# A two-layer transformer block on one core: the experts' TensorE order pinned, weight splits of 2048 columns in three buffers

## The chip, the cores and the metric

The kernel runs on one core of a Trainium2 chip. The metric is the device time of one execution in microseconds (us), as the median of several runs. A NeuronCore has five engines that run side by side and wait for one another through semaphores: PE (TensorE, matrix products), DVE (VectorE), ACT (ScalarE), POOL (GpSimd) and SP (SyncE, which here only starts transfers). Transfers run on 16 DMA engines.

## The reference

Two layers over 256 tokens of 1024 features, all in fp32. Layer 0 is a stick-breaking attention and a dense SwiGLU of 2816 hidden features; layer 1 is a block attention (with 256 tokens there is one block, so it is a causal softmax with a relative bias) and a mixture of 8 experts, top 2, each a SwiGLU of 3584 hidden features. Cut to its core:

```
for i in range(2):
    hn = rmsnorm(h, mixer_norm[i]);  q, k, v = heads(hn @ w_qkv[i])
    o = stick_breaking_attention(q, k, v) if i == 0 else moba_attention(q, k, v, rel_bias)
    h = h + o @ w_o[i]
    hn = rmsnorm(h, ffn_norm[i])
    if i == 0: h = h + (silu(hn @ w1) * (hn @ w3)) @ w2
    else:      # gates: softmax over the two largest of hn @ router
        h = h + sum_e gate[:, e] * ((silu(hn @ e_w1[e]) * (hn @ e_w3[e])) @ e_w2[e])
return rmsnorm(h, final_norm)
```

## The kernel before, in words

**Three products for one.** TensorE multiplies in a reduced form of fp32. To keep fp32 accuracy each weight is split in two: ACT copies it into the reduced form (L154, `wh`) and DVE subtracts that from the weight (L155, `wl`). `mm3` (L175 to 179) then makes three matmuls: L176 `wh` by the high part of the data, L177 `wl` by the high part, L178 `wh` by the low part. The data are the stationary operand, the weights stream through as 512 columns. The data are split in the same way by `split_out` (L182 on ACT, L183 on DVE).

**The weights' way.** A list `jobs` holds all weights in the order of use, as granules of 128 x 2048 elements (1 MB). SP loads them into a ring of buffers (`RING` = 9 and, in the expert stage, 7 more that other stages have freed). `stream` takes a loaded granule, makes the two splits in pieces of `HALF` = 1024 columns, and yields 512-column slices to `mm3`. The pieces lie in a pool `split` with four buffers for `wh` and four for `wl`. A buffer is written again when the last matmul that reads it is done, and a ring slot is loaded again when its split is done. Weights that take a norm's factor (`g` not None: qkv and the dense w1 and w3) are split 512 columns at a time by L162 and L163.

**An expert.** Its rows (at most 128 are computed here, the rest is left to code behind a branch at the end) pass through 7 chunks of 512 hidden features, so the stage has 56 chunks. A chunk, by the loop at the end of the listing, is: w1, two granules (called G0 and G1 below), into one bank; w3, two granules (G2, G3), into another; ACT's silu (L587) and DVE's product (L588) make the hidden tile `nat`; and the w2 product (`down`) of the chunk before, two granules (G4, G5). Before that product `hid_t` turns the hidden tile of the chunk before by four transposes (L599), and `split_out` writes it into the single pair of buffers `hts`. A chunk is thus 72 matmuls of 512 columns and 4 transposes. At the last chunk of an expert `turn_x` adds 8 transposes (L876) with a split of the next expert's rows, and in the first chunk of the next one `store_y` copies the result out (ACT L859, DVE L860). In the last expert `fetch` gathers the others' results and `add_rows` (L847, four instructions of 1024 columns on DVE) adds them to `h`.

**Who sets the order.** The Tile framework's scheduler lays out each engine's queue from the dependences; `behind` adds an order without a semaphore where the author wants one. Each engine then works its queue strictly in order. In the experts before, nothing but the scheduler says where the transposes L599 stand among TensorE's matmuls.

**Ahead of the experts** stands the routing: after the last `w_o` matmul, `h` gets the attention's output (L534), TensorE turns it (L287) and multiplies by the router (L695), with copies on ACT (L742) and DVE (L740), the router's logits leave the bank by L704, and a chain of small DVE steps up to L714 and L865 gives the order in which TensorE gathers each expert's rows (L887).

## Time and profile before

| | |
|---|---|
| runs, median (lowest to highest) | 1440.25 us (1438.56 to 1440.41), 3 runs |
| the profiled execution: its time, its span | 1438.46 us, 1436.8 us |
| granted TensorE clock over the span | 0.996 |
| PE busy | 1417.6 us, 99% of the span |
| DVE, ACT, POOL busy | 1170.2 us (81%), 1010.3 us (70%), 45.3 us (3%) |
| moved by DMA | 442.11 MB, 308 GB/s in the mean |

A row of the timeline gives the start (us from the span's start), the time of the row, engine, line, operation, what is written from what, tile and data type, and how many instructions the row takes together. Behind it, in brackets, stands the time for which the engine had been idle and the instruction that ended the wait. Since matmuls are pipelined, the time between two starts tells more than the time of one. The share of busy time is a mean: the experts take 960 of the 1437 us, and what one wait there costs is read from that stage.

### The profile page before, as it was taken

The numbers are of one execution on the slowest core, as the hardware profiler recorded it, in microseconds if no ns is written. First come the engines' busy times: TensorE is split into PE (matmuls) and PEld (weight loads), VectorE is DVE, ScalarE is ACT, GpSimd is POOL, SyncE is SP. The second block draws the span as 40 slices with busy tenths as digits, with TensorE's granted clock in tenths as the row PEclk, the third lists the DMA queues.
The fourth block names the chain that finished last, engine by engine and source line by source line (L and its number), as shares of the span: only waits on it lengthen the run. The fifth ranks groups of instructions, "written<-read, shape, count | busy, mean of one in ns | idle before, by whom it ended". The sixth has DMA issues, their size and how long they took to land. (4 is left out here: it accounts for less than half of the span.)

```text
span 1436.8 us, 19637 instructions
## 1 busy us (share of the span) xinstructions
PE 1417.6 (99%) x7285; PEld 1176.7 (82%) x7285; DVE 1170.2 (81%) x1384; ACT 1010.3 (70%) x1282; POOL 45.3 (3%) x71
## 2 busy tenths in 40 slices
PE   9999999999999999999999999999999999999997
PEld 7877999988877888888888888878878887887775
DVE  6656766667667999999999988888888888898887
ACT  6656655546655778878878777777777777777765
POOL 1000000000001000000000000000000000000200
PEclk9999999999999999999999999999999999999998
DMA  9633865556566999999999999999999999999850
GB/s 353 236 117 108 303 196 186 186 173 228 180 246 218 402 401 388 385 373 373 388 392 362 391 362 373 366 381 368 354 389 372 357 380 380 358 374 369 320 189 32
DMA packets 172153, 442.11 MB, mean 308 GB/s; under 512 B 7299, under 2 KB 9395, under 8 KB 157972
## 3 DMA queue, kind: packets, MB, share of 16 engines
q1 hardware_dynamic: 166852, 422.61, 80.6%
q0 software_dynamic: 5136, 18.18, 3.5%
q8 instruction: 59, 0.97, 0.3%
q14 instruction: 42, 0.34, 0.1%
q10 hardware_dynamic: 64, 0.02, 0.0%
HBM read 430.00 MB, written 11.03 MB: 307 GB/s over the span
## 5 line engine op out<-in xcount | busy, mean ns | idle before, releaser
L155 DVE TENSOR_TENSOR wl<-raw,wh 128x1024 fp32r<-128x1024 f32 x710 | 834.4, 1220 | 112.9 <-ACT wh L154 106.0
L154 ACT ACTIVATE wh<-raw 128x1024 fp32r<-128x1024 f32 x710 | 725.6, 1057 | 133.9 <-PE bank L178 97.7
L177 PE MATMUL bank<-wl,oh_t 128*128 128x512 f32 x968 | 382.9, 396 | 2.9 <-DVE wl L155 2.0
L176 PE MATMUL bank<-wh,oh_t 128*128 128x512 f32 x968 | 375.5, 393 | 2.1 <-ACT wh L154 1.6
L178 PE MATMUL bank<-wh,oh_t 128*128 128x512 f32 x904 | 353.5, 391 | 0.1
L177 PEld LDWEIGHTS bank<-wl,oh_t 128*128 128x128 f32 x968 | 181.9, 188 | 60.0 <-DVE wl L155 18.9
L176 PEld LDWEIGHTS bank<-wh,oh_t 128*128 128x128 f32 x968 | 182.2, 188 | 41.4 <-ACT wh L154 1.8
L178 PEld LDWEIGHTS bank<-wh,oh_t 128*128 128x128 f32 x904 | 170.2, 188 | 34.1 <-DVE oh_t L183 0.8
L178 PE MATMUL bank<-wh,ol_t 128*128 128x512 f32 x504 | 194.6, 392 | 0.0
L162 ACT ACTIVATE wh<-raw,gcol 128x512 fp32r<-128x512 f32 (+1 forms) x192 | 123.8, 698 | 87.4 <-PE bank L318 56.3
L163 DVE SCALAR_TENSOR_TENSOR wl<-raw,gcol,wh 128x512 fp32r<-128x512 f32 (+1 forms) x192 | 131.1, 725 | 65.8 <-ACT wh L162 65.3
L177 PE MATMUL bank<-wl,ol_t 128*128 128x512 f32 x440 | 174.7, 397 | 0.4 <-DVE wl L155 0.4
L318 PE MATMUL bank<-x_h,wh 128*128 128x256 f32 x512 | 143.8, 282 | 0.0
L318 PE MATMUL bank<-x_h,wl 128*128 128x256 f32 x512 | 142.9, 280 | 0.0
L318 PE MATMUL bank<-x_l,wh 128*128 128x256 f32 x512 | 142.7, 279 | 0.0
L176 PE MATMUL bank<-wh,ol_t 128*128 128x512 f32 x440 | 137.1, 393 | 0.0
L178 PEld LDWEIGHTS bank<-wh,ol_t 128*128 128x128 f32 x504 | 94.4, 188 | 19.9 <-issue 1.1
L318 PEld LDWEIGHTS bank<-x_h,wh 128*128 128x128 f32 x512 | 95.9, 188 | 1.9 <-issue 1.1
L177 PEld LDWEIGHTS bank<-wl,ol_t 128*128 128x128 f32 x440 | 83.0, 189 | 16.4 <-DVE wl L155 0.6
L318 PEld LDWEIGHTS bank<-x_h,wl 128*128 128x128 f32 x512 | 96.1, 188 | 0.0
L318 PEld LDWEIGHTS bank<-x_l,wh 128*128 128x128 f32 x512 | 95.9, 187 | 0.2
L176 PEld LDWEIGHTS bank<-wh,ol_t 128*128 128x128 f32 x440 | 81.6, 188 | 16.8
(218 smaller groups left out, 1106.1 us busy)
## 6 DMA issues: line engine op xcount, KB each, us to landing
raw<-in_e_w_dram SPq DMA_DIRECT2D x335, 1024.0 KB, 7.3
raw<-in_w_dram SPq DMA_DIRECT2D x33, 1024.0 KB, 5.1
raw<-in_w_qkv_dram SPq DMA_DIRECT2D x22, 1024.0 KB, 5.7
raw<-in_w_o_dram SPq DMA_DIRECT2D x8, 1024.0 KB, 7.5
xs_d<-hn POOLq DMA_DIRECT2D x1, 4096.0 KB, 16.0
xr<-xs_d POOLq DMA_DIRECT2D x7, 512.0 KB, 7.5
ys_d<-yr POOLq DMA_DIRECT2D x7, 512.0 KB, 7.8
raw<-in_w_qkv_dram SPq DMA_DIRECT2D x4, 512.0 KB, 6.8
```

The source lines that it names most:

```text
L154: i0 = nc.scalar.activation(wh[:, :m], src, AF.Copy)
L155: i1 = nc.vector.tensor_sub(wl[:, :m], src, wh[:, :m].bitcast(F32))
L162: i0 = nc.scalar.activation(wh[:, cs], src[:, cs], AF.Copy, scale=gc)
L163: i1 = nc.vector.scalar_tensor_tensor(wl[:, cs], src[:, cs], gc, wh[:, cs].bitcast(F32), op0=ALU.mult, op1=ALU.subtract)
L176: i0 = nc.tensor.matmul(ps, s[0], m[0], start=start, stop=False)
L177: nc.tensor.matmul(ps, s[0], m[1], start=False, stop=False)
L178: i1 = nc.tensor.matmul(ps, s[1], m[0], start=False, stop=stop)
L318: nc.tensor.matmul(to, w[a][:, ms], z[:, :, c], start=c + i + m % 2 == 0, stop=c == NC - 1 and m % 2 == 1 and i == 2, skip_group_check=True)
```

## The change

The order of TensorE in the experts is written with `behind`: each group of matmuls is placed after the last of the group before (`last`), so that the order of a chunk is w1, the four transposes, w3, (the turn of the next rows), w2. Weights without a norm factor (`w_o`, the dense w2, all of the experts') are split in pieces of 2048 columns, a granule at once, and the pieces lie in three tiles of 2048 columns for `wh` and three for `wl`; weights with a factor still go in halves of such a tile. The ring gives up two slots for it. All other queues (ACT, DVE, POOL, SP) are still laid out by the scheduler. Lines move: L154 and L155 become L166 and L167, L176 to L178 become L188 to L190, L182 and L183 become L194 and L195, L587 and L588 become L599 and L600, L599 becomes L611, L847 becomes L864 and L860 becomes L877.

```diff
--- before.py
+++ after.py
@@ -30,9 +30,10 @@
 BIG = 1e30
 N_BUCKETS = 32
 MAX_DISTANCE = 128
-RING = 9
+RING = 7
 RING1, RING2, RING3 = 1, 3, 3
 GRAN = 2048
+SPLITS = 3
 HALF = GRAN // 2
 NV = 384
 WARM = 6
@@ -50,7 +51,19 @@
 
     const = ctx.enter_context(tc.tile_pool(name="const", bufs=1))
     ring = ctx.enter_context(tc.tile_pool(name="ring", bufs=RING))
-    split = ctx.enter_context(tc.tile_pool(name="split", bufs=4))
+    split = ctx.enter_context(tc.tile_pool(name="split", bufs=1))
+    highs, lows = ([split.tile([P, GRAN], F32R, name=f"{n}{i}") for i in range(SPLITS)]
+                   for n in ("wh", "wl"))
+    n_split = [0]
+
+    def next_split(m):
+
+        if n_split[0] % GRAN + m > GRAN:
+            n_split[0] += -n_split[0] % GRAN
+        at, i = n_split[0] % GRAN, n_split[0] // GRAN
+        n_split[0] += m
+        return [x[i % SPLITS][:, at:at + m] for x in (highs, lows)]
+
     act = ctx.enter_context(tc.tile_pool(name="act", bufs=1))
     small = ctx.enter_context(tc.tile_pool(name="small", bufs=2))
     psp = ctx.enter_context(tc.tile_pool(name="psp", bufs=1, space=PSUM))
@@ -144,11 +157,10 @@
             t = loaded[n_used[0]]
             _, nk, fn = jobs[n_used[0]]
             n_used[0] += 1
-            k = min(nk, HALF // fn)
+            k = min(nk, (GRAN if g is None else HALF) // fn)
             for c0 in range(0, nk, k):
-                wh = split.tile([P, HALF], F32R, name="wh")
-                wl = split.tile([P, HALF], F32R, name="wl")
                 m = k * fn
+                wh, wl = next_split(m)
                 src = t[:, c0 * fn:c0 * fn + m]
                 if g is None:
                     i0 = nc.scalar.activation(wh[:, :m], src, AF.Copy)
@@ -592,18 +604,23 @@
                                            op1=ALU.mult)
         return t
 
-    def hid_t(t, n, ps, a, c, apart=True):
+    def hid_t(t, n, ps, a, c, apart=True, after=None):
         k = n // P
         tv = t[:, :n].rearrange("p (f j) -> p j f" if apart else "p (j f) -> p j f", j=k)
         for j in range(k):
-            nc.tensor.transpose(ps[:, j * P:(j + 1) * P], tv[:, j], ident)
+            i0 = nc.tensor.transpose(ps[:, j * P:(j + 1) * P], tv[:, j], ident)
+            if after is not None:
+                behind((i0, after))
+                after = i0
         split_out(ps[:, :n], a[:, :n], c[:, :n])
         return [(a[:, j * P:(j + 1) * P], c[:, j * P:(j + 1) * P]) for j in range(k)]
 
-    def down(ps, hT, j, w, start, stop):
+    def down(ps, hT, j, w, start, stop, after=None):
         for half in range(2):
-            mm3(ps[half], hT[j], tuple(a[:, half * FC:(half + 1) * FC] for a in w),
-                start and j == 0, stop and j == len(hT) - 1)
+            i0, i1 = mm3(ps[half], hT[j], tuple(a[:, half * FC:(half + 1) * FC] for a in w),
+                         start and j == 0, stop and j == len(hT) - 1)
+            behind((i0, after))
+        return i1
 
     def dense_ffn(pool, hold, then):
         y = [[bank[0], bank[1]], [bank[2], bank[7]]]
@@ -933,7 +950,7 @@
                 i1 = nc.vector.tensor_add(ht[b][:, hs], ht[b][:, hs], ps)
         return i0, i1
 
-    pend, done, added = None, None, None
+    pend, done, added, last = None, None, None, None
     gather((3, 4), raws[2])
     k = 0
     most_v = None
@@ -947,15 +964,18 @@
                 if bk == b3:
                     held[:] = None, None
                 for c, w in enumerate(stream(NC, hold=held)):
-                    _, last = mm3(bank[bk], (eh[:, c], el[:, c]), w, c == 0, c == NC - 1)
+                    i0, i1 = mm3(bank[bk], (eh[:, c], el[:, c]), w, c == 0, c == NC - 1)
+                    behind((i0, last))
+                last = i1
                 if pend is not None and bk == b1:
-                    hT = hid_t(pend[1], FC, bank[pend[2]], *hts)
+                    hT = hid_t(pend[1], FC, bank[pend[2]], *hts, after=last)
             if i == len(ecs) - 1 and e + 1 < NE:
                 turn_x(xr, (2, 7), last)
             t = gate_mul(ep.tile([P, FC], F32, name="nat"), bank[b1], bank[b3], n, after=added)
             if pend is not None:
                 for j, w in enumerate(stream(4)):
-                    down(y, hT, j, w, pend[0] == 0, pend[0] == len(ecs) - 1)
+                    i1 = down(y, hT, j, w, pend[0] == 0, pend[0] == len(ecs) - 1, last)
+                last = i1
             pend = (i, t, b1)
             if i == 0:
                 if e:
```

The order of TensorE in one chunk, before: `ol_t` is the turned hidden tile of the w2 product, bank_76 and bank_77 take its result.

```order
L177 MATMUL bank_76<-wl,ol_t 128x512
L178 MATMUL bank_76<-wh,ol_t 128x512
L177 MATMUL bank_77<-wl,ol_t 128x512
L178 MATMUL bank_77<-wh,ol_t 128x512
L176 MATMUL bank_76<-wh,ol_t 128x512
L176 MATMUL bank_77<-wh,ol_t 128x512
L599 MATMUL bank_79<-ident,nat 128x128 x4
L177 MATMUL bank_76<-wl,ol_t 128x512
L178 MATMUL bank_76<-wh,ol_t 128x512
L177 MATMUL bank_77<-wl,ol_t 128x512
```

After, at the same place of the program (bank_87 is the w1 product, bank_88 the w3 product):

```order
L189 MATMUL bank_87<-wl_69,oh_t 128x512
L190 MATMUL bank_87<-wh_66,oh_t 128x512
L611 MATMUL bank_85<-ident,nat 128x128 x4
L188 MATMUL bank_88<-wh_67,oh_t 128x512
L189 MATMUL bank_88<-wl_70,oh_t 128x512
L190 MATMUL bank_88<-wh_67,oh_t 128x512
L188 MATMUL bank_88<-wh_67,oh_t 128x512
```

The four transposes stood among the w2 product of the chunk before; now they stand between w1 and w3 of the same chunk.

DVE's order in a chunk of the later experts, before: each raw buffer (a granule) gives two pieces, and the product L588 stands between the two pieces of the first w2 granule and those of the second.

```order
L155 TENSOR_TENSOR wl_10421<-raw_10061,wh_10420 128x1024
L155 TENSOR_TENSOR wl_10431<-raw_10061,wh_10430 128x1024
L588 TENSOR_TENSOR nat_10415<-nat_10415,bank6_82 128x512
L155 TENSOR_TENSOR wl_10443<-raw_10089,wh_10442 128x1024
L155 TENSOR_TENSOR wl_10453<-raw_10089,wh_10452 128x1024
L155 TENSOR_TENSOR wl_10465<-raw_10111,wh_10464 128x1024
L155 TENSOR_TENSOR wl_10475<-raw_10111,wh_10474 128x1024
L183 TENSOR_TENSOR ol_t_90<-bank5_81,ol_t_90 128x512
L155 TENSOR_TENSOR wl_10487<-raw_10136,wh_10486 128x1024
```

After (wl0 to wl2 are the three tiles): the rows from G3 of a chunk to G0 of the next.

```order
L167 TENSOR_TENSOR wl0_68<-raw_8425,wh0_65 128x2048
L195 TENSOR_TENSOR ol_t_96<-bank3_85,ol_t_96 128x512
L167 TENSOR_TENSOR wl1_69<-raw_8441,wh1_66 128x2048
L600 TENSOR_TENSOR nat_8667<-nat_8667,bank6_88 128x512
L167 TENSOR_TENSOR wl2_70<-raw_8460,wh2_67 128x2048
L167 TENSOR_TENSOR wl0_68<-raw_8476,wh0_65 128x2048
```

A granule is one row now. From the third expert's fourth chunk on the product L600 stands ahead of the whole G5, as here, where in the chunks before it stands behind G5.

DVE's order around the last chunks of expert 7, before (L847 is `add_rows`):

```order
L155 TENSOR_TENSOR wl_12456<-raw_12094,wh_12455 128x1024
L155 TENSOR_TENSOR wl_12466<-raw_12122,wh_12465 128x1024
L847 SCALAR_TENSOR_TENSOR h0_84<-raw_12056,ex_4567,h0_84 128x1024
L155 TENSOR_TENSOR wl_12476<-raw_12122,wh_12475 128x1024
L847 SCALAR_TENSOR_TENSOR h0_84<-raw_12056,ex_4567,h0_84 128x1024
L588 TENSOR_TENSOR nat_12442<-nat_12442,bank6_82 128x512
L847 SCALAR_TENSOR_TENSOR h1_85<-raw_12064,ex_4567,h1_85 128x1024
L183 TENSOR_TENSOR ol_t_90<-bank5_81,ol_t_90 128x512
L155 TENSOR_TENSOR wl_12488<-raw_12144,wh_12487 128x1024
L847 SCALAR_TENSOR_TENSOR h1_85<-raw_12064,ex_4567,h1_85 128x1024
```

After, from G0 of the chunk before the last on; wl0 of raw_9884 is that chunk's G0, wl0 of raw_9954 its G3, raw_9916 G1 and raw_9932 G2:

```order
L167 TENSOR_TENSOR wl0_68<-raw_9884,wh0_65 128x2048
L864 SCALAR_TENSOR_TENSOR h0_90<-raw_9900,ex_4271,h0_90 128x1024 x2
L864 SCALAR_TENSOR_TENSOR h1_91<-raw_9908,ex_4271,h1_91 128x1024
L167 TENSOR_TENSOR wl0_68<-raw_9954,wh0_65 128x2048
L864 SCALAR_TENSOR_TENSOR h1_91<-raw_9908,ex_4271,h1_91 128x1024
L167 TENSOR_TENSOR wl1_69<-raw_9916,wh1_66 128x2048
L167 TENSOR_TENSOR wl2_70<-raw_9932,wh2_67 128x2048
```

And the last chunk, where raw_10005 is G0, raw_10021 G1, raw_10059 G3 and raw_10037 G2:

```order
L600 TENSOR_TENSOR nat_10194<-nat_10194,bank6_88 128x512
L167 TENSOR_TENSOR wl0_68<-raw_10005,wh0_65 128x2048
L167 TENSOR_TENSOR wl1_69<-raw_10021,wh1_66 128x2048
L167 TENSOR_TENSOR wl0_68<-raw_10059,wh0_65 128x2048
L167 TENSOR_TENSOR wl2_70<-raw_10037,wh2_67 128x2048
L167 TENSOR_TENSOR wl1_69<-raw_10075,wh1_66 128x2048
```

G3 moved ahead of G1 and G2 into the tile that G0 has just left, with three of the four additions ahead of it; in the last chunk G3 moved ahead of G2. ACT's queue has the same order of pieces. TensorE's has G0, G1, the transposes, G2, G3 in both chunks.

DVE in the routing before (sums, a norm's step, the copy of the turned rows, the logits):

```order
L534 TENSOR_TENSOR h0_84<-h0_84,bank0_76 128x512
L534 TENSOR_TENSOR h0_84<-h0_84,bank1_77 128x512
L534 TENSOR_TENSOR h1_85<-h1_85,bank2_78 128x512
L534 TENSOR_TENSOR h1_85<-h1_85,bank7_83 128x512
L277 TENSOR_SCALAR ms_4484<-ss_4482 128x1
L740 COPY hn1_148<-bank6_82 128x512
L704 COPY lg_3319<-bank0_76 128x8
```

After (L546, L289, L757 and L721 are L534, L277, L740 and L704):

```order
L546 TENSOR_TENSOR h0_90<-h0_90,bank0_82 128x512
L546 TENSOR_TENSOR h0_90<-h0_90,bank1_83 128x512
L546 TENSOR_TENSOR h1_91<-h1_91,bank2_84 128x512
L546 TENSOR_TENSOR h1_91<-h1_91,bank7_89 128x512
L167 TENSOR_TENSOR wl1_69<-raw_3846,wh1_66 128x2048
L757 COPY hn1_154<-bank6_88 128x512
L289 TENSOR_SCALAR ms_4188<-ss_4186 128x1
L721 COPY lg_3095<-bank0_82 128x8
```

The piece of raw_3846 (G2 of expert 0's first chunk) now stands between the sums and the copies; on ACT its `wh` stands ahead of the copies L759 (L742 of before).

## Rows read from the trace of the kernel before

**Rows 1.** The page, busy time of each engine and its share.

```profile
PE 1417.6 (99%) x7285; PEld 1176.7 (82%) x7285; DVE 1170.2 (81%) x1384; ACT 1010.3 (70%) x1282; POOL 45.3 (3%) x71
```

**Rows 2.** DVE timeline, the product L588: one in each chunk.

```profile
476.72 0.68 DVE L588 TENSOR_TENSOR nat<-nat,bank 128x512 f32<-128x512 f32 x1
...
629.17 0.68 DVE L588 TENSOR_TENSOR nat<-nat,bank 128x512 f32<-128x512 f32 x1
629.77 4.92 DVE L155 TENSOR_TENSOR wl<-raw,wh 128x1024 fp32r<-128x1024 f32 x4
...
646.01 0.68 DVE L588 TENSOR_TENSOR nat<-nat,bank 128x512 f32<-128x512 f32 x1
...
972.07 0.68 DVE L588 TENSOR_TENSOR nat<-nat,bank 128x512 f32<-128x512 f32 x1
...
989.22 0.68 DVE L588 TENSOR_TENSOR nat<-nat,bank 128x512 f32<-128x512 f32 x1
...
1354.48 0.69 DVE L588 TENSOR_TENSOR nat<-nat,bank 128x512 f32<-128x512 f32 x1 [1.77 <-PE bank L178]
...
1413.06 0.68 DVE L588 TENSOR_TENSOR nat<-nat,bank 128x512 f32<-128x512 f32 x1
```

**Rows 3.** ACT timeline, the chunk from 957 us on.

```profile
960.26 0.60 ACT L182 ACTIVATE ol_t<-bank 128x512 fp32r<-128x512 f32 x1 [1.95 <-PE bank L177]
```

**Rows 4.** Waits of the weight loads, 466 to 1413 us: total us, times, longest.

```profile
PEld bank L177 <- DVE wl L155: 19.3, 44, 1.1
```

**Rows 5.** Timeline of PE, PEld and DVE at one such wait.

```profile
961.84 1.23 DVE L155 TENSOR_TENSOR wl<-raw,wh 128x1024 fp32r<-128x1024 f32 x1 [0.26 <-ACT wh L154]
...
963.01 0.39 PE L176 MATMUL bank<-wh,oh_t 128*128 128x512 f32 x1
963.12 0.19 PEld L177 LDWEIGHTS bank<-wl,oh_t 128*128 128x128 f32 x1
963.24 0.40 PE L177 MATMUL bank<-wl,oh_t 128*128 128x512 f32 x1
```

**Rows 6.** PE timeline, the turn of the next expert's rows.

```profile
559.85 1.03 PE L876 MATMUL bank<-ident,xr 128*128 128x128 f32 x8
560.64 0.71 PE L176 MATMUL bank<-wh,ol_t 128*128 128x512 f32 x2
```

**Rows 7.** The costliest groups: busy us, mean ns, idle before and releaser.

```profile
L155 DVE TENSOR_TENSOR wl<-raw,wh 128x1024 fp32r<-128x1024 f32 x710 | 834.4, 1220 | 112.9 <-ACT wh L154 106.0
L154 ACT ACTIVATE wh<-raw 128x1024 fp32r<-128x1024 f32 x710 | 725.6, 1057 | 133.9 <-PE bank L178 97.7
```

**Rows 8.** PE and DVE timeline, the last w_o matmuls and the sums.

```profile
437.47 0.62 PE L178 MATMUL bank<-wh,ol_t 128*128 128x512 f32 x2
...
437.90 2.48 DVE L534 TENSOR_TENSOR h<-h,bank 128x512 f32<-128x512 f32 x4 [1.88 <-PE bank L178]
...
438.38 0.62 PE L178 MATMUL bank<-wh,ol_t 128*128 128x512 f32 x2
```

**Rows 9.** ACT and DVE timeline, the copies and the logits of the routing.

```profile
439.47 1.09 ACT L742 ACTIVATE hn<-bank 128x512 f32<-128x512 f32 x2 [3.91 <-PE bank L287]
...
442.75 0.17 DVE L704 COPY lg<-bank 128x8 f32<-128x8 f32 x1 [0.20 <-PE bank L695]
```

**Rows 10.** DVE timeline, an addition of rows in expert 7 and its successor.

```profile
1393.89 1.28 DVE L847 SCALAR_TENSOR_TENSOR h<-raw,ex,h 128x1024 f32<-128x1024 f32 x1
1395.08 0.68 DVE L588 TENSOR_TENSOR nat<-nat,bank 128x512 f32<-128x512 f32 x1
```

**Rows 11.** PE timeline, the longest wait of expert 7's end.

```profile
1398.19 0.50 PE L176 MATMUL bank<-wh,oh_t 128*128 128x512 f32 x1 [1.63 <-ACT wh L154]
```

**Rows 12.** Windows behind it: busy PE, PEld, DVE, ACT, POOL, PEclk, DMA.

```profile
1400.00:1402.00 2.00, 2.00 (x6) 1.17 (x5) 2.00 (x3) 1.47 (x3) 0.00 (x0) 0.52 0.00 0
1402.00:1404.00 2.00, 2.00 (x6) 1.63 (x7) 2.00 (x3) 0.57 (x1) 0.00 (x0) 0.63 0.00 0
```

**Rows 13.** SP's waits: us in total, times, longest one.

```profile
SPq L130 <- DVE wl L155: 863.7, 332, 10.0
```

## The prediction

> **What bounds the kernel now.** I read the page's busy times first: PE is busy for 1417.6 us, 99% of the span, DVE for 81% and ACT for 70% [rows 1]. A gain can come only from time in which TensorE stands still or runs slowly, so I looked next at how long a chunk of the experts takes. Its clock is the DVE product, one in each chunk [rows 2]. From 629.17 to 646.01 a chunk takes 16.84 us. The matmuls of one half product start 0.2275 us apart (four from 437.47 to 438.38 [rows 8]); 72 of them make 16.38, and with four transposes a chunk has nothing left to lose at 16.84. From 972.07 to 989.22 it takes 17.15 [rows 2]. The whole run of 54 chunks from 476.72 to 1413.06 takes 936.34; 54 x 16.84 are 909.36, so 27.0 us are lost there. This sum is what the change can work on.
>
> Where they go: seven turns of the next expert's rows belong to the work and stay. Eight transposes take 0.79 to the next matmul, and the two matmuls behind take 0.71 instead of 0.62, together 0.88 [rows 6]; seven are 6.2. The last three chunks, from 1354.48 to 1413.06, take 58.58 instead of 50.52: 8.1 lost [rows 2]. The other 12.7 lie mostly in the chunks of 17.15. There ACT waits 1.95 us with the split of the turned hidden tile [rows 3]: the transposes are done early, inside the w2 product of the chunk before, but the single buffer `hts` is read until that product's last matmul. What ACT splits behind it is late, then DVE, and in the end the weight load of the second product: 44 such waits, 19.3 us [rows 4].
>
> **Prices.** A 1024-column subtraction takes 1.22 us, ACT's copy 1.06 [rows 7]. The trace has no 2048-column one. Between the 512-column row of 0.68 [rows 2] and 1.22 lie 0.54 for 512 columns, so 1024 more cost 1.08 and a piece of 2048 takes 2.30. From above it is bounded by two pieces, 2.44; from below by four times the 0.54, 2.16, as if starting cost nothing. I take 2.30, the line through two rows. For ACT, 0.60 at 512 columns [rows 3] and 1.06 give 1.98. A DVE instruction lets its successor start about 0.09 before its end (0.68 after 0.60, 629.17 to 629.77 [rows 2]; 1.28 after 1.19 [rows 10]), so a piece holds the queue for 2.21. TensorE's last matmul lets DVE begin 0.43 after its start (437.47 to 437.90 [rows 8]). DVE's piece ends at 961.84 + 1.23 = 963.07 and the waiting weight load starts at 963.12, 0.05 later, which is 0.11 after the start of the matmul in front (963.01). The next matmul starts 0.23 after that one, as usual [rows 5]. So a weight load may come 0.11 late without cost, and beyond it every delay counts.
>
> **The order of TensorE.** With the transposes behind w1, the w2 product that read `hts` is over before them, so ACT's wait goes. What is late next is G5's low part, wherever L600 stands ahead of the whole G5 in DVE's queue. Let the last matmul of G3 start at 0. L600 starts at 0.43, G5's subtraction at 1.03, it ends at 3.33, the weight load can start at 3.38. G4's 12 matmuls and the first two of G5 start in between; the second of these two starts at 14 x 0.227 = 3.18, and the load may come until 3.29. It is 0.09 late. With a piece of 1024 columns the same step had 1.0 to spare. This holds for 32 chunks, from the third expert's fourth on, without the chunks that hold a turn, whose transposes give 0.88 of slack, and the last two: 32 x 0.09 = 2.9. In the earlier chunks L600 stands behind G5 and the cost is nothing.
>
> **Ends of experts.** In the same order two splits of the turned rows stand between G5 and the next G0 (2 x 0.60). G0's subtraction runs from 1.03 + 2.21 + 1.20 = 4.44 to 6.74, its load could start at 6.79. The matmul in front starts after 0.88 + 25 x 0.227 = 6.56, so the load is due at 6.67: 0.12 late. One chunk on, the copy out (L877) waits for the last w2 matmul (24 x 0.227 + 0.09 + 0.43 = 5.97), and G1's subtraction follows from 6.57 to 8.87, its load at 8.92; due is 37 x 0.227 + 0.09 + 0.11 = 8.60: 0.32 late. Five of the seven ends have this order: 5 x 0.44 = 2.2.
>
> **The routing.** ACT's copy of G2 waits for the last `w_o` matmul (438.61), so it runs from 439.04 to 441.02, ahead of the copy that started at 439.47 [rows 8, 9]. DVE's piece holds its queue from 441.06 to 443.27; then L757 (0.60) and a small step (0.08), and the logits are read at 443.95 instead of 442.75 [rows 9]. The chain behind them ends at the gathers, so TensorE begins the experts 1.2 later.
>
> **The end of expert 7.** G3 of the last chunk but one goes into the tile that G0 has left. Let G0's first matmul start at 0; its piece entered DVE's queue at -2.5 and leaves it at -0.3. Three additions of 1.19 [rows 10] end at 3.3 and are covered. ACT's copy for G3 waits for G0's last matmul (11 x 0.227 + 0.43 = 2.93), ends at 4.91; the subtraction holds DVE until 7.2, the fourth addition until 8.35, and only then G1's subtraction runs, until 10.65. TensorE wants it at 2.72 + 0.11: 7.8 us of standing still. In the last chunk G3 stands ahead of G2 in the same way. From the start of G0's last matmul on: 0.43, 1.98 on ACT, 2.21 for G3, 2.30 for G2 and 0.1 of signals make 7.0; G1 and the transposes cover 13 x 0.227 + 0.5 + 0.1 = 3.6: 3.4 us. After such a wait the clock falls: behind the 1.63 us wait and a further one [rows 11], 2 us at 0.52 and 2 us at 0.63 [rows 12], that is from the upper level of 2.4 GHz to 1.2 for most of 3.4 us, and 2 x 0.48 + 2 x 0.37 = 1.7 lost. I count it once. Together 12.9, against 8.1 now.
>
> The Trainium skill says of the clock (TensorE: Matmul & The Clock Gate, HAM oscillation) that every long enough wait throttles the array anew. By it the second wait would cost another 1.7; rows 11 and 12 agree for the first, and no row here shows two in turn.
>
> **What costs nothing.** Pieces of `w_o` and the dense w2 lie beside a TensorE that is idle for 19 us in the whole span [rows 1]; there is little to win in those stages, and I allow 1 us either way. Two ring slots less: SP waits 863.7 us, 332 times, for a split to free a slot [rows 13], so the ring is full ahead of use; 14 slots are some 39 us of work at 16.84 per six. If that cover were gone, each wait of TensorE for a load would show on L166.
>
> **Sum.** Of the 27.0, the turns keep 6.2. The other 20.8 go; 2.9 + 2.2 + 1.2 + 12.9 = 19.2 come. The profiled execution of 1438.46 becomes 1436.9. The median of the runs, 1440.25, stands 1.8 above that execution, the lowest run beside it. I place the median of the changed kernel between, at 1438.3: no change that can be told, since a measurement of this kernel tells about 0.2%, 2.9 us.
>
> **Rivals.** First, faster: the 0.09 is thin. If a piece takes 2.20 instead of 2.30, the 32 waits go (2.9), the ends cost 0.2 each less (1.2), the end of expert 7 some 0.4: 1433.8. A cheaper end of expert 7 works the same way, up to 4 us. For it speaks that 0.43 and 0.05 are single rows; against it, that 2.20 lies under the line of rows 2 and 7.
>
> The Trainium skill gives this rival a rule and its opposite (VectorE: DVE Perf Modes, The TRN2 errata): a fixed term of 58 cycles at 0.96 GHz in one table, which makes 2.19 of 2048 columns, and 151 measured for such a two-operand fp32 operation, which makes 2.29. For 1024 columns they give 1.13 and 1.22; the trace has 1.220 and decides for the second. I leave the first a tenth within this rival's chance.
>
> Second, slower: a piece costs as much as two, 2.44. Then G5 is 0.23 late, 32 times (4.5 more), G0 and G1 at the ends 0.28 more (1.4), the end of expert 7 some 0.6, the routing 0.1: 1444.9. It decides from about 2.40 on, where the sum passes 2.9 over the old median. Against it stands the same line; for it, that three buffers of a granule leave nothing to hide a late piece.
>
> Third, the order doesn't cure: the split of the hidden tile still waits for something else in the later experts and chunks stay at 17.15. Then the 12.7 don't go, the 2.9 don't come: 1448. Against it: the transposes come after the w2 product in TensorE's own queue.
>
> **How the numbers follow.** My forecast gets 0.38 (its own range 1436 to 1442), the first rival 0.37, the second 0.19, the third 0.06. So faster 0.37, within 0.2% 0.38, slower 0.25. The range takes in the first rival with the cheaper end, 1430, and the second with a little of the third, 1446.5.
>
> **What would show it.** Chunks of 16.84 in experts 0 and 1 and about 16.93 later; L167 at 2.30; ACT's L194 without its wait; a wait of TensorE of about 7 to 8 us in expert 7's last chunk but one on DVE's G1, another of 3 in the last. I am wrong if later chunks take 17 or more, if the end of expert 7 runs through, or if TensorE waits in the attention or the dense stage.

## The result: 1447.56 us, slower by half a per cent

The changed kernel takes 1447.56 us (median of four runs, 1443.66 to 1447.94) against 1439.40 of the kernel before in the same job (1438.18 to 1440.41): a ratio of 1.0052, interval 1.0039 to 1.0064. The forecast was 1438.3 with a range up to 1446.5. The profiled execution took 1447.67 us, its span 1445.9; before, span 1436.8. The 9.1 us between the spans are what has to be found. One of the four executions took 1443.66, with a granted clock of 0.993 over its span instead of 0.991, so what the clock costs differs from one to the next. (One execution of the last kernel below took 1749.17 us at a granted clock of 0.75; it belongs to the chip's slow state, and its ratio leaves it out.)

The page of the changed kernel, busy times and the two costliest groups (line, engine, operation, count | busy us, mean ns of one | idle before, releaser). Its L166 and L167 are L154 and L155 of before:

```profile
PE 1415.8 (98%) x7285; PEld 1181.5 (82%) x7285; DVE 1140.0 (79%) x1030; ACT 970.0 (67%) x928; POOL 46.2 (3%) x71
...
L167 DVE TENSOR_TENSOR wl<-raw,wh 128x2048 fp32r<-128x2048 f32 (+1 forms) x356 | 805.9, 2283 | 155.0 <-ACT wh L166 154.3
L166 ACT ACTIVATE wh<-raw 128x2048 fp32r<-128x2048 f32 (+1 forms) x356 | 676.4, 1914 | 261.7 <-PE bank L190 214.9
```

DVE and ACT are 30 and 40 us less busy than in [rows 1], because half as many split instructions start; the time is longer all the same. A piece costs 2.28 us on DVE and 1.91 on ACT, where 2.30 and 1.98 were forecast. Two pieces of 1024 cost 2.44 [rows 7].

**Where the 9.1 us are.** The experts are cut at the first matmul and at the DVE products (one in each chunk; L588 before [rows 2], L600 now). PE and DVE timeline of the changed kernel, the last `w_o` matmul, the first of the experts, the product that begins the last three chunks, and the last product:

```profile
440.30 0.39 PE L188 MATMUL bank<-wh,oh_t 128*128 128x512 f32 x1
...
455.08 0.50 PE L188 MATMUL bank<-wh,oh_t 128*128 128x512 f32 x1
...
1349.83 0.69 DVE L600 TENSOR_TENSOR nat<-nat,bank 128x512 f32<-128x512 f32 x1 [0.27 <-PE bank L190]
...
1417.28 0.68 DVE L600 TENSOR_TENSOR nat<-nat,bank 128x512 f32<-128x512 f32 x1
```

The same instants before were 437.92, 452.96, 1354.48 and 1413.06. So:

| stretch | before | after | difference | forecast |
|---|---|---|---|---|
| to the last high part of `w_o` (L176 before, L188 now) | 437.9 | 440.3 | +2.4 | 0 |
| routing, to the first expert matmul | 15.0 | 14.8 | -0.3 | +1.2 |
| chunks, to the last three | 901.5 | 894.8 | -6.8 | -7.6 |
| the last three chunks | 58.6 | 67.5 | +8.9 | +4.8 |
| from the last product to the end | 23.7 | 28.6 | +4.9 | 0 |

The differences are taken from the instants themselves, before rounding.

**The chunks** came out as worked out, though not for the reason given, as the experiments show. DVE timeline of the changed kernel, two products of expert 4, against [rows 2]:

```profile
972.74 0.69 DVE L600 TENSOR_TENSOR nat<-nat,bank 128x512 f32<-128x512 f32 x1 [0.28 <-PE bank L190]
973.35 6.69 DVE L167 TENSOR_TENSOR wl<-raw,wh 128x2048 fp32r<-128x2048 f32 x3
...
989.69 0.69 DVE L600 TENSOR_TENSOR nat<-nat,bank 128x512 f32<-128x512 f32 x1 [0.27 <-PE bank L190]
```

A late chunk takes 16.95 instead of 17.15. The two ends of an expert take 17.84 and 17.29 (differences of products, the same in four experts): 1.45 above two chunks of 16.84, of which 0.88 is the turn and 0.57 the lateness.

**The end of expert 7** is where the gain goes. ACT, DVE and PE timeline of the changed kernel:

```profile
1375.04 5.51 ACT L166 ACTIVATE wh<-raw 128x2048 fp32r<-128x2048 f32 x3 [6.34 <-PE bank L190]
```

```profile
1371.79 3.80 DVE L864 SCALAR_TENSOR_TENSOR h<-raw,ex,h 128x1024 f32<-128x1024 f32 x3
1376.98 2.29 DVE L167 TENSOR_TENSOR wl<-raw,wh 128x2048 fp32r<-128x2048 f32 x1 [1.40 <-ACT wh L166]
1379.19 1.28 DVE L864 SCALAR_TENSOR_TENSOR h<-raw,ex,h 128x1024 f32<-128x1024 f32 x1
1380.39 4.49 DVE L167 TENSOR_TENSOR wl<-raw,wh 128x2048 fp32r<-128x2048 f32 x2
```

```profile
1372.12 0.39 PE L188 MATMUL bank<-wh,oh_t 128*128 128x512 f32 x1
...
1378.80 0.79 PE L188 MATMUL bank<-wh,oh_t 128*128 128x512 f32 x1 [3.80 <-ACT wh L166]
1382.73 0.79 PE L189 MATMUL bank<-wl,oh_t 128*128 128x512 f32 x1 [3.13 <-DVE wl L167]
...
1388.60 0.40 PE L189 MATMUL bank<-wl,oh_t 128*128 128x512 f32 x1
...
1408.71 0.78 PE L189 MATMUL bank<-wl,oh_t 128*128 128x512 f32 x1 [2.23 <-DVE wl L167]
```

The order is the one forecast: G3's piece goes first (DVE, 1376.98), the fourth addition follows, and G1, which TensorE wants next, comes at 1380.39. From G0's first matmul at 1372.12 the first low part of G1 is due at 1375.07 (13 x 0.227); it runs at 1382.73, 7.66 late (7.8 forecast). In the last chunk the same way makes 3.27 (3.4 forecast; 2.23 of it stands in the row, the rest is the wait in front of it). But the clock costs more than was allowed. Windows of the changed kernel (busy us and counts of PE, PEld, DVE, ACT, POOL; then PEclk, DMA share, GB/s):

```profile
1386.00:1388.00 2.00, 2.00 (x7) 1.51 (x6) 0.00 (x0) 0.18 (x1) 0.00 (x0) 0.50 0.00 0
...
1410.00:1412.00 2.00, 2.00 (x6) 1.52 (x6) 1.46 (x2) 0.00 (x0) 1.00 (x1) 0.50 0.00 0
```

Behind the first wait the matmuls start 0.43 apart up to 1388.3, at 0.50 of the clock, the lower level of 1.2 GHz. Set beside the same instructions of an earlier chunk, 2.65 us are lost from 1382.73 to 1388.60. Behind the second wait it is 1.67. So TensorE loses 7.66 + 2.65 + 3.27 + 1.67 = 15.25 at this end. (The remaining 1.7 of the 67.45 - 50.52 = 16.9 in the table is mostly the last product's own place: it stands behind a piece in DVE's queue and starts 1.9 after the last `w3` matmul, where the product at 1349.83 starts 0.4 after it.)

**Behind the last product** nothing had been forecast. PE timeline around the branch that skips the second half of the rows, of the kernel before and then of the changed one:

```profile
1422.54 0.39 PE L176 MATMUL bank<-wh,oh_t 128*128 128x512 f32 x1
1423.77 0.47 PE L177 MATMUL bank<-wl,oh_t 128*128 128x512 f32 x1 [0.84 <-PEq L1063]
```

```profile
1423.21 0.40 PE L189 MATMUL bank<-wl,oh_t 128*128 128x512 f32 x1
1426.69 0.76 PE L190 MATMUL bank<-wh,oh_t 128*128 128x512 f32 x1 [3.08 <-PEq L1083]
```

TensorE's sequencer stands at the branch 3.08 us instead of 0.84: four matmuls are left between the last transposes and the branch, where before 23 covered it. The experiments below show that this comes with the three tiles of the split and not with TensorE's written order. Then 14 matmuls from 1426.69 to 1432.74 take 6.05 us instead of 3.2 (14 x 0.227), again at half clock. 2.2 + 2.9 make the 4.9 and a little.

**The routing** forecast was half right: the logits are read at 446.22 instead of 442.75 [rows 9], 1.1 more than the 2.4 by which `w_o` ends later. But the products behind them run at full clock now. A window of before, while its gathers ran, then one of the changed kernel:

```profile
448.00:450.00 2.00, 2.00 (x12) 1.94 (x11) 1.83 (x11) 0.00 (x0) 0.16 (x1) 0.50 0.03 9
```

```profile
452.00:454.00 2.00, 1.57 (x15) 1.42 (x14) 2.00 (x18) 0.00 (x0) 0.16 (x1) 1.00 0.00 0
```

Before, the clock was at 0.50 here and at 0.71 in the next window; now it is at 1.00 throughout. With that the 1.1 is back, and a little more. That the change keeps the clock up here is not shown: the kernel that differs from the one before only by a ring of 7 runs the same matmuls with the clock at 1.00 in these windows too, and takes 14.0 us for the stretch, 1.0 less than before and 0.8 less than the changed kernel. At a like clock the change costs 0.8 here, against the 1.2 forecast.

**Before the experts** 2.4 us are new, and 1.6 of them lie in the last attention, from 404 us on, where TensorE has no wait in either kernel. PE timeline, score products of one pair of heads, before and then in the changed kernel:

```profile
406.49 0.49 PE L468 MATMUL bank<-kT,qT 64*128 64x128 f32 x4
406.82 0.60 PE L471 MATMUL bank<-kT,qT 64*128 64x256 f32 x4
```

```profile
405.06 0.49 PE L480 MATMUL bank<-kT,qT 64*128 64x128 f32 x2
405.39 0.59 PE L483 MATMUL bank<-kT,qT 64*128 64x256 f32 x2
```

A head's product uses 64 rows of the array. Before, the two heads of a pair stand next to each other, and eight instructions take 0.86 us (406.49 to the next at 407.35; two at a time start 0.007 us apart). In the changed kernel five matmuls of other products stand between the heads, two of them of `w_o`; the four instructions of one head take 0.85 (405.06 to 405.91), and those of the other as much again from 407.27 on. Two pairs are parted in this way that were not before: 1.7 us. The change writes nothing of this order; it comes out of the scheduler, with other pieces and other buffers for `w_o`. The Trainium skill (TensorE: Matmul & The Clock Gate, Why this matters for your kernels) states that products with few rows in distinct row groups run at the same time; the rows agree. The rest of the 2.4 is 0.3 of a later start, which differs from run to run, and some 0.4 in the stages between.

### The profile page after: what moved, and what is told of

It is laid out like the page before. It is cut to its first block, busy times and chain, and to the rows that moved or that the text cites. A ratio compares the mean times of both kernels' runs of the same rounds, so it can differ in the third digit from the quotient of the medians.

```text
span 1445.9 us, 18586 instructions
## 1 busy us (share of the span) xinstructions
PE 1415.8 (98%) x7285; PEld 1181.5 (82%) x7285; DVE 1140.0 (79%) x1030; ACT 970.0 (67%) x928; POOL 46.2 (3%) x71
## 5 line engine op out<-in xcount | busy, mean ns | idle before, releaser
L167 DVE TENSOR_TENSOR wl<-raw,wh 128x2048 fp32r<-128x2048 f32 (+1 forms) x356 | 805.9, 2283 | 155.0 <-ACT wh L166 154.3
L166 ACT ACTIVATE wh<-raw 128x2048 fp32r<-128x2048 f32 (+1 forms) x356 | 676.4, 1914 | 261.7 <-PE bank L190 214.9
L188 PE MATMUL bank<-wh,oh_t 128*128 128x512 f32 x968 | 385.9, 399 | 5.6 <-ACT wh L166 4.4
L190 PE MATMUL bank<-wh,oh_t 128*128 128x512 f32 x904 | 355.9, 394 | 3.1 <-PEq L1083 3.1
L188 PEld LDWEIGHTS bank<-wh,oh_t 128*128 128x128 f32 x968 | 184.1, 190 | 43.1 <-ACT wh L166 5.0
L190 PEld LDWEIGHTS bank<-wh,oh_t 128*128 128x128 f32 x904 | 171.5, 190 | 40.4 <-issue 3.5
L190 PE MATMUL bank<-wh,ol_t 128*128 128x512 f32 x504 | 192.3, 392 | 0.0
L174 ACT ACTIVATE wh<-raw,gcol 128x512 fp32r<-128x512 f32 (+1 forms) x192 | 129.3, 703 | 78.7 <-PE bank L330 42.7
L189 PE MATMUL bank<-wl,ol_t 128*128 128x512 f32 x440 | 171.3, 396 | 0.0
L188 PE MATMUL bank<-wh,ol_t 128*128 128x512 f32 x440 | 154.0, 391 | 0.0
L190 PEld LDWEIGHTS bank<-wh,ol_t 128*128 128x128 f32 x504 | 94.4, 188 | 19.7 <-issue 1.4
L188 PEld LDWEIGHTS bank<-wh,ol_t 128*128 128x128 f32 x440 | 82.1, 188 | 17.0
```

Source lines behind the costliest of these rows:

```text
L166: i0 = nc.scalar.activation(wh[:, :m], src, AF.Copy)
L167: i1 = nc.vector.tensor_sub(wl[:, :m], src, wh[:, :m].bitcast(F32))
L174: i0 = nc.scalar.activation(wh[:, cs], src[:, cs], AF.Copy, scale=gc)
L188: i0 = nc.tensor.matmul(ps, s[0], m[0], start=start, stop=False)
L189: nc.tensor.matmul(ps, s[0], m[1], start=False, stop=False)
L190: i1 = nc.tensor.matmul(ps, s[1], m[0], start=False, stop=stop)
```

## The experiments

Theory A: the written order and the pieces of 2048 each do what was worked out, and the loss is the end (expert 7's inverted order, the clock behind it, the branch). Rivals: one half of the change is good and the other bad (B), or the ring of 7 costs (C). Each ratio is against the kernel before in the same job: 1439.16 in the first, 1437.60 in the second, 1439.53 in the third.

### The halves of the change

**Only the order of TensorE, with pieces of 1024, four buffers and a ring of 9.**

```
-    def down(ps, hT, j, w, start, stop):
+    def down(ps, hT, j, w, start, stop, after=None):
...
+            behind((i0, after))
...
-                    hT = hid_t(pend[1], FC, bank[pend[2]], *hts)
+                    hT = hid_t(pend[1], FC, bank[pend[2]], *hts, after=last)
```

> The kernel before with TensorE's order of the experts written down, and nothing else of the change (pieces of 1024, four buffers, ring of 9). Theory (the order cures the chunks of 17.15, and the larger pieces and the smaller ring cost what the change loses): every chunk without a turn takes 16.84, 12.7 us less before the last three chunks; the additions stand around G0 of the last chunk now and make its G1 about 3.5 us late, so the end loses 4 to 6 instead of 8.1; together 1423 to 1427. Rival (the order of TensorE itself brings the loss, for instance by the transposes that stand in front of w3): chunks above 16.9, 1440 or more.

Measured: 1446.96 us, ratio 1.0044 (1.0027 to 1.0060), so slower. Late chunks take 17.52 instead of 17.15. My theory fell here. ACT timeline, PE timeline, and the waits for weight loads of this kernel:

```profile
1004.23 0.60 ACT L182 ACTIVATE ol_t<-bank 128x512 fp32r<-128x512 f32 x1 [2.13 <-PE bank L599]
1004.72 0.59 ACT L587 ACTIVATE nat<-bank 128x512 f32<-128x512 f32 x1
1005.20 4.90 ACT L154 ACTIVATE wh<-raw 128x1024 fp32r<-128x1024 f32 x5
```

```profile
1003.56 0.63 PE L599 MATMUL bank<-ident,nat 128*128 128x128 f32 x4
...
1007.57 0.50 PE L177 MATMUL bank<-wl,oh_t 128*128 128x512 f32 x1 [0.39 <-DVE wl L155]
```

```profile
PEld bank L177 <- DVE wl L155: 31.3, 36, 3.8
```

The wait of [rows 3] doesn't go: ACT now waits 2.13 for the transposes instead of 1.95 for the product. The piece behind the split is copied at 1005.20 and wanted by TensorE 4.0 - 0.4 = 3.6 us after the transposes. The changed kernel has the same wait. Its ACT and PE timeline:

```profile
984.20 0.60 ACT L194 ACTIVATE ol_t<-bank 128x512 fp32r<-128x512 f32 x1 [1.27 <-PE bank L611]
984.69 0.59 ACT L599 ACTIVATE nat<-bank 128x512 f32<-128x512 f32 x1
985.17 3.72 ACT L166 ACTIVATE wh<-raw 128x2048 fp32r<-128x2048 f32 x2
```

```profile
983.53 0.63 PE L611 MATMUL bank<-ident,nat 128*128 128x128 f32 x4
```

There the piece in front of the split holds 12 matmuls instead of six, so the piece behind it is wanted later, and TensorE doesn't wait for it: between 983.53 and 989 no matmul comes late that isn't so in a chunk of 16.84 too. The 0.11 of the late chunks lies at G5.

**Only the pieces of 2048 in three buffers, with a ring of 7; TensorE's order left to the scheduler.**

```
-                    behind((i0, last))
...
-                    hT = hid_t(pend[1], FC, bank[pend[2]], *hts, after=last)
+                    hT = hid_t(pend[1], FC, bank[pend[2]], *hts)
...
-                    i1 = down(y, hT, j, w, pend[0] == 0, pend[0] == len(ecs) - 1, last)
+                    down(y, hT, j, w, pend[0] == 0, pend[0] == len(ecs) - 1)
```

> The changed kernel without TensorE's written order (pieces of 2048 in three buffers and the ring of 7 stay). Theory (with pieces of 2048 the scheduler's queues on ACT and DVE let the chunk run whichever place the transposes have; the written order adds nothing then): late chunks of 16.84 to 16.95, the same inverted pieces at the end of expert 7 and the same tail, 1445 to 1449. Rival (the written order is what takes the chunk from 17.15 to 16.95): late chunks of 17.1 or more, 1452 or more.

Measured: 1469.37, ratio 1.0203 (1.0186 to 1.0220). The rival was right on the time and wrong on the place. Plain chunks take 16.84, less than in the changed kernel, but behind four of the seven turns two chunks take 18.8 and 19.0 (20.4 once), the first chunk of all 14.5 instead of 10.9, and the last three 67.6. Waits of the experts in this kernel:

```profile
PE bank L189 <- DVE wl L167: 21.4, 11, 3.5
PE bank L188 <- ACT wh L166: 7.3, 4, 3.8
```

I read it so: three buffers leave no piece in hand where TensorE's order and that of the copies differ. That is a reading and not shown. With pieces of 2048 in three tiles the written order is worth 22 us, and with pieces of 1024 in four buffers it costs 8.

**Pieces of 1024, two in each of the three buffers; the rest as changed.**

```
-            k = min(nk, (GRAN if g is None else HALF) // fn)
+            k = min(nk, HALF // fn)
```

> The changed kernel with pieces of 1024 columns in the same three tiles, so six halves; TensorE's order and the ring of 7 stay. Theory (the pieces of 2048 make the 0.11 us a chunk and 0.45 at the ends of experts, some 6 us, while the order at the end of expert 7 comes from the ring of 7 with TensorE's order): chunks of 16.84 throughout, the last three chunks still above 64 us and the tail still 28.6; about 1441. Rival (the long waits at the end come from the pieces of 2048): the last three chunks at 58 or less and the whole below 1432.

Measured: 1465.02, ratio 1.0170 (1.0153 to 1.0187), 24 more than expected. Late chunks of 17.52 as in the order alone: between this kernel and the changed one only the size of the piece differs, and it makes 17.52 or 16.95. The last three take 65.3, so the inverted order at expert 7's end doesn't hang on the size of the pieces. Waits in the experts:

```profile
PEld bank L189 <- DVE wl L167: 33.6, 36, 4.8
```

**The order, pieces of 1024, and the split of the hidden tile held behind G3's pieces.** The edit on top of the first of these kernels:

```
-        split_out(ps[:, :n], a[:, :n], c[:, :n])
+        if after is None:
+            split_out(ps[:, :n], a[:, :n], c[:, :n])
...
+            if pend is not None:
+                i0, i1 = split_out(bank[pend[2]], *hts)
+                behind((i0, piece[0]), (i1, piece[1]))
```

> The second experiment's kernel (the kernel before with TensorE's order alone, 1447, late chunks of 17.5) with the split of the turned hidden tile held behind the pieces of the second w3 granule on ACT and DVE. Theory (in the late chunks the scheduler puts that split, which waits for the transposes behind w1, ahead of the second w3 granule on ACT, and everything behind it comes 0.68 late): chunks of 16.84 to 17.0 in the late experts, about 33 of them 0.55 to 0.68 shorter, 1425 to 1430. Rival (pieces of 1024 with this order are late for the product L588 or for the two-piece release): chunks stay at 17.5, 1445 or more.

Measured: 1440.03, ratio 1.0001 (0.9992 to 1.0011). Late chunks take 17.11: 0.41 of the 0.68 come back. So ACT's order is most of what makes the order alone slow, and not all; DVE's low part still holds the loads up:

```profile
PEld bank L179 <- DVE wl L156: 25.8, 67, 4.4
```

**Only the ring of 7.**

```
-RING = 9
+RING = 7
```

> The kernel before with a ring of 7 instead of 9 buffers (14 slots instead of 16 in the experts), nothing else. Theory (the ring is full ahead of use, so two slots cost nothing by themselves): 1439.4, within 2 us, and TensorE's waits as before. Rival (the ring's loss makes loads late or holds transfers behind the additions): 1443 or more, with waits of ACT on a transfer or for slots near the end.

Measured: 1439.78, ratio 1.0001 (0.9992 to 1.0011). C is out, as far as the ring alone goes; a larger ring beside the three tiles was not run.

**What these kernels show of the end.** The branch's wait and the inverted order come neither from TensorE's order nor from the size of the pieces. The branch's wait with the order alone (four buffers), and with the pieces of 2048 alone (three tiles):

```profile
PE bank L177 <- PEq L1071: 0.8, 1, 0.8
```

```profile
PE bank L190 <- PEq L1081: 3.3, 1, 3.3
```

With pieces of 1024 in the three tiles it is 3.4. From the last product to the end the four kernels with four buffers take 23.7 to 24.1 us, the three with three tiles 28.1 to 28.6, whichever order and size they have. The order of the pieces goes the same way. When TensorE's long waits for DVE end in the last two chunks, DVE has subtracted a piece or more ahead of its turn in the three kernels with three tiles (67.5, 67.6 and 65.3 us for the last three chunks) and none in the four others (57.6 to 60.0). The change needs the three tiles for its large pieces; the ring of 7, which goes with them, does none of this by itself. Why the scheduler lays out the end in another way with them is not shown.

### The end of expert 7 and what follows it

In the kernels that follow, `piece` is the last pair of split instructions.

**The pieces of expert 7 held in the order of the stream.**

```
+                    if pinned[0]:
+                        behind((i0, piece[0]), (i1, piece[1]))
+                    piece[:] = i0, i1
...
+        pinned[0] = e == NE - 1
```

> The changed kernel, with ACT's and DVE's pieces of expert 7 held in the order in which TensorE uses them (G0, G1, G2, G3), nothing else. Theory (the order of the pieces at the end of expert 7 makes the two long waits there, 7.8 and 3.25 us in the changed kernel's profile, and the slow clock behind them 5.8 us): no wait in the last chunk; in the last but one the four additions still stand ahead of G1, which makes G1 about 4 us late, with 1.7 to 2.7 us of slow clock behind it; the last three chunks take about 57 to 58 us instead of 67.5, the whole about 1438. The tail behind the last product stays at 28.6 us. Rival (the additions or late transfers make the waits, not the order of the pieces): the waits stay at about 11 us in total and the time at 1447.

Measured: 1437.41, ratio 0.9987 (0.9977 to 0.9996), against 1.0052 without it. The last three chunks take 58.9 instead of 67.5: chunks of 16.84 and 16.95 and one of 25.1. What is left there is the four additions, which stand together ahead of G1's low part:

```profile
PE bank L193 <- DVE wl L168: 4.4, 2, 3.9
PE bank L194 <- PEq L1088: 3.6, 1, 3.6
```

The branch's wait stays (3.08 in the changed kernel). The next three edits are each put on this kernel.

**The additions spread, two in each of the last two chunks, behind G2's and G4's pieces.**

```
+                    if e == NE - 1 and i >= 5 and bk == b3 and c == 3:
+                        add_rows(i - 5, came[i - 5], 0)
...
+                    if e == NE - 1 and i >= 5 and j == 1:
+                        add_rows(i - 5, came[i - 5], 1)
...
-                elif i in (4, 5):
-                    added = add_rows(i - 4, came[i - 4])
```

> The first experiment's kernel with the four additions of rows in expert 7 apart: two in each of the last two chunks, each behind a different granule's low part. Theory (four additions in a row, 4.8 us, make G1 late by 4 and the clock falls behind that wait): the last three chunks fall from 58.9 to 51.5 or 52.5 us, no wait above 0.5 us and no slow clock there; 1430 to 1431. Rival (the wait is for gathered rows or transfers): a wait of 3 us or more remains at the first addition, 1436 or more.

The product of a chunk is no longer held behind the additions either. Measured: 1431.30, ratio 0.9956 (0.9939 to 0.9972). The last three chunks take 53.2 from product to product; TensorE loses next to nothing in them (0.1 at G5, twice), the rest of the 2.7 over 50.5 is the products' place.

**The pieces pinned in all experts, and the product behind the last piece of its chunk.**

```
-        pinned[0] = e == NE - 1
+        pinned[0] = True
...
+            t = gate_mul(ep.tile([P, FC], F32, name="nat"), bank[b1], bank[b3], n, after=added)
+            behind((mul[0], piece[1]))
```

> The first experiment's kernel with every DVE product of a chunk placed behind the low parts of the w2 granules beside it (in all experts as the scheduler has it in the first three). Theory (the 0.11 us of each later chunk is the product standing ahead of the second w2 granule's subtraction): chunks of 16.84 in the later experts too, 32 times 0.11 less, and 0.1 less at five ends of experts; 1433 to 1434. Rival (the 0.11 comes from the size of the piece on ACT, or from the buffers): the later chunks stay at 16.95, the time at 1437.

Measured: 1433.66, ratio 0.9968 (0.9956 to 0.9979). Late chunks take 16.84, the two at an expert's end 17.75 and 17.16. In a late chunk of the changed kernel the matmul behind G5's first low part starts 0.31 us after it, and here 0.23 like the others. So the lateness (0.09 forecast, 0.11 measured) is, as forecast, the product L600 standing ahead of G5's low part. (The pins and the product's place were not tried apart.)

**The branch's load behind the last product of the first half.**

```
-    most_v = nc.values_load(most_i[0:1, 0:1], min_val=0, max_val=S)
+    for j, w in enumerate(stream(4)):
+        _, i1 = mm3(y[0], hT[j], w, False, j == 3)
+    loads, (most_v,) = nc.values_load_multi_w_load_instructions(most_i[0:1, 0:1], min_val=0,
+                                                                max_val=S)
+    behind(*((x, i1) for x in loads if x.ins.engine == mybir.EngineType.PE))
```

> The first experiment's kernel (expert 7's pieces in stream order) with the branch of the tail held on TensorE behind all 14 matmuls of the last w2 half that can run, where the changed kernel has 4 in front of it. Theory (the branch takes TensorE some 4 us from the last wait on, whatever stands in front, and the matmuls in front hide it, as the 20 of before did; with few in front the clock falls as well): the tail from the last product to the end falls from 28.6 to 24 to 25.5 us, the whole from 1437.4 to 1433 or 1434. Rival (the tail is longer for the later arrival of the last granules or of the hidden tile): tail still above 27.5, time 1436.5 or more.

Measured: 1434.30, ratio 0.9977 (0.9967 to 0.9986). From the last product to the end 24.8 us instead of 27.9. TensorE still stands there for 2.1 us, but the clock stays up. PE timeline and a window of this kernel:

```profile
1417.13 0.47 PE L194 MATMUL bank<-wh,oh_t 128*128 128x512 f32 x1 [2.08 <-PEq L1092]
```

```profile
1418.00:1420.00 2.00, 2.00 (x11) 1.61 (x10) 0.00 (x0) 0.29 (x1) 0.00 (x0) 1.00 0.00 0
```

**All three.** The four edits above in one kernel. As in the kernel of the spread additions, `add_rows` takes the half as an argument and enters the chain of pieces:

```
+        behind((i0, piece[1]))
+        piece[1] = i0
```

> The three together: branch late, products last, additions apart. Theory (the three losses lie in different places and add up): 1437.4 less 4, 4 and 7, some 1422 to 1424, with chunks of 16.84 in all experts. Rival (they overlap, since the clock or the transfers take back what is gained): 1428 or more.

Measured: 1425.08 us (1424.05 to 1425.19), ratio 0.9909 (0.9892 to 0.9925). This beats both kernels: 12.5 us under the kernel before in the same job, and 22.5 under the changed kernel's median, which is of another job. It is 1 us above what was expected. DVE timeline of the last chunk but one, and the longest wait of PE from 466 us on; what waits are left take 0.7 or less:

```profile
1372.25 1.28 DVE L870 SCALAR_TENSOR_TENSOR h<-raw,ex,h 128x1024 f32<-128x1024 f32 x1
1373.45 4.49 DVE L168 TENSOR_TENSOR wl<-raw,wh 128x2048 fp32r<-128x2048 f32 x2
1377.85 1.28 DVE L870 SCALAR_TENSOR_TENSOR h<-raw,ex,h 128x1024 f32<-128x1024 f32 x1
```

```profile
PE bank L194 <- PEq L1098: 2.1, 1, 2.1
```

**The same, with pieces of 1024 in `w_o` and the dense stage**, to see whether the 2.4 us ahead of the experts come from the size of the pieces there.

```
-            k = min(nk, (GRAN if g is None else HALF) // fn)
+            k = min(nk, (GRAN if experts[0] else HALF) // fn)
```

> The eighth experiment's kernel (all three mends) with pieces of 2048 in the experts only, and 1024 for w_o and the dense w2. Theory (the 2.4 us by which the changed kernel is behind at the end of layer 1's attention come from the pieces of 2048 among the attention's and the norm's steps): TensorE is at the router's turn at 439 instead of 441, 1422 to 1424. Rival (they come from another order of the scheduler that the piece size does not decide): 1425, within 1 us.

Measured: 1429.54, ratio 0.9930 (0.9910 to 0.9950), against 0.9909 (0.9892 to 0.9925) with 2048 throughout: not faster, and the intervals overlap. `w_o` ends at 444.5, later still. Of the 4.7 by which it is later than in the kernel of all three edits, 1.1 is the start and some 3 are lost between 64 and 158 us, of which about 1 comes back up to 388; the last attention loses another 1.6, though one more pair of heads stands together there again. So the smaller piece alone is no cure, and the heads are not all that decides that stage; with three buffers instead of four, the scheduler's order differs from that of the kernel before in either case. What would restore both stages was not tried.

## Why the prediction was wrong

**What held.** The piece: 2.28 against 2.30 (the Trainium skill's fixed term of 151 cycles, VectorE: DVE Perf Modes, The TRN2 errata, makes 2.29; the other table's 2.19 is not what this operation takes). Late chunks: 16.95 against 16.93. Ends of experts: 0.57 against 0.44 and the 0.09 of one late chunk. Both waits of expert 7: 7.66 and 3.27 against 7.8 and 3.4. The ring: nothing. The first rival, that 0.09 is thin, fell: the lateness came. The second, a piece as dear as two, fell too. The third, that the order doesn't cure, is not what this kernel shows (16.95, not 17.15), but the order alone shows it.

**The step that failed** is, before all, where the sum ends. It stopped at the last product and put everything behind it at nothing, without a reason: it cost 4.9 us, by the trace 2.2 of wait at TensorE's branch and 2.9 of clock behind it. Moving the branch's load gave 3.1 back. What takes away the matmuls that covered the branch is the three tiles of the split (0.8 to 1.2 us of wait with four buffers, 3.1 to 3.4 with three tiles), and not the written order, which alone leaves the tail at 23.7. The order of the changed kernel shows the branch with four matmuls in front of it, so this could have been read beforehand.

**The clock at expert 7's end, "I count it once",** is the second term that failed. It fell twice: 2.65 + 1.67 = 4.3 instead of 1.7. The Trainium skill's rule that every long enough wait throttles anew (TensorE: Matmul & The Clock Gate, HAM oscillation), by which the prediction worked out another 1.7 and left it out of its sum, agrees with the second fall: 1.67. The first was dearer than the price taken from [rows 11, 12], and the length of the wait doesn't explain it: in two kernels with the same wait of 3.93 us there, 2.6 and 1.7 were lost behind it.

**"What costs nothing"** allowed 1 us either way ahead of the experts and asked only what covers the pieces of `w_o` and the dense stage, not what new pieces and buffers do to the scheduler's order of TensorE: +2.4, of which 1.6 came in the last attention, where heads no longer stand side by side. In the twelve profiles beside that of the kernel before the pairs go with pieces and buffers: the three kernels with pieces of 1024 and four buffers keep both pairs, the seven with pieces of 2048 there keep none, and the two with pieces of 1024 in three tiles keep one. That it is the cause is read from the rows; no run changed it alone, and the last kernel above loses the 1.6 there with a pair kept.

**A term that was too dear.** The routing's 1.2 came back through the clock, since the gathers behind it ran at 1.00 instead of 0.50 and 0.71. That is luck as far as the runs show: the program of before, with a ring of 7, ran them at 1.00 as well.

Together, by the differences of the table from their forecasts: 2.4 - 1.5 + 0.8 + 4.1 + 4.9 = 10.7, the way from the forecast -1.6 to +9.1. Of the 4.1 at the end, 2.6 are the clock and -0.3 the waits; the rest is for the most part the place of the last products and not time of TensorE.

**A reason that was right by luck.** The 12.7 us were said to go because the order ends ACT's wait. ACT's wait did not go at all: in the changed kernel it waits 37 times for the transposes, up to 1.6 us, and the sign "ACT's L194 without its wait" was wrong. The order alone made chunks slower (17.52). The pieces of 2048 alone brought plain chunks to 16.84 and lost more than that behind the turns (1469.4). Beside the written order it is the larger piece that takes the late chunk from 17.52 to 16.95; that it does so because the piece in front of the split keeps TensorE busy for longer is read from the rows.

**What stays open.** Why three tiles make the scheduler lay out the end and the attention in another way, why the order with 1024 columns stops at 17.11 when ACT's split is held back, and what part of the 2.4 us would come back if the heads were held together.

## What to carry to other kernels

Price an edit of order or buffers to its end: follow every engine's queue to the last instruction, and ask at each wait or branch there how many matmuls still stand in front of it. Run the parts of a change apart, the buffers too: what looked like the work of the written order here came with the three tiles. Price a TensorE wait together with the clock behind it, each time anew, as a range. An order written on one engine leaves the engines that feed it to the scheduler: here the two halves of a change cost 8 and 30 us apart, and with the feeding order, the additions and the branch written down too they gained 12.5.

## What the runs showed of the hardware

The clock's price does not follow from the length of the wait. The kernel with the pieces of expert 7 in the order of the stream and the one that also moves the branch's load have the same wait in expert 7's last chunk but one, 3.93 us for DVE; the row of the second:

```profile
1377.80 0.73 PE L193 MATMUL bank<-wl,oh_t 128*128 128x512 f32 x1 [3.93 <-DVE wl L168]
```

Behind it matmuls start 0.43 apart for 3.5 us here, and for 4.9 us in the other; the chunks take 24.2 and 25.1. With the 2.65 and 1.67 of the changed kernel, and 2.9 behind its branch, one fall of the clock with matmuls close behind it cost 1.7 to 2.9 us in this case.

The clock did not fall behind every wait, either. Behind the 2.08 us at the branch, in the kernel that moves the branch's load, the window from 1418 us shows 1.00, and the kernel of all three edits shows the same behind its 2.1. Behind 2.23 us in the changed kernel's last chunk, with a shorter wait in front of it, it fell to 0.50.

A busy TensorE can lose time that no view names: eight instructions that run in 0.86 us where two heads of 64 rows stand together take 1.7 where they don't, without any idle time.
